# A hybrid state-space and attention layer on one core: three queues put into the written order

## The chip, the cores and the metric

The kernel runs on one core of one Trainium2 chip. A core has five instruction queues that run beside each other: TensorE (PE, matrix multiplications, with its weight loads listed as PEld), VectorE (DVE), ScalarE (ACT), GpSimd (POOL) and SyncE (SP). SP does no arithmetic here: it issues nearly all transfers (DMA) between the memory of the chip and the core's own buffers. An instruction that has to wait for another engine or for a transfer holds up everything behind it in its queue. The metric is the device time of one execution in microseconds (us).

## The reference

One layer of a streaming encoder, sequence length 2048, width 1024, all float32:

```python
h = rmsnorm(x, norm_mix_g)
proj = h @ w_in 
y_ssm = s5_mixer(u_ssm, ...)
y_att = chunked_attention(q, k, v, attn_rel_bias)
mixed = concat([rmsnorm(y_ssm, g1), rmsnorm(y_att, g2)])
x = x + mixed @ w_out
h2 = rmsnorm(x, norm_ffn_g)
x = x + (silu(h2 @ w_gate) * (h2 @ w_up)) @ w_down
return rmsnorm(x, norm_final_g)
```

The state-space mixer has 32 groups of 16 channels with 64 complex states each, scanned in time, followed by GELU and a gate. The attention has 8 heads of 64 dimensions; a frame sees its own chunk of 64 frames and the 8 chunks before it, with a learned bias by distance.

## The kernel before

Products of float32 are made from three products of a rounded high part and a low remainder (hi times hi, hi times lo, lo times hi). So every operand is split: ACT casts the high part, DVE or POOL subtracts it to get the low part (the function `split`).

The program has these phases: a prologue that projects u and prepares the state-space tables; the attention stage (`att_phase`), which is what the change touches; the mixing phase with w_out; gate and up projections; the down projection.

The attention stage is written as 128 steps: four quarters of the sequence (`sb`, 512 frames each), four pairs of heads (`pr`), two heads (`hh`), four blocks of queries (`qp`). `ORDER = "sptf"` says what a step writes: the scores of this step with the row minimum and the exponential ("s"; scores carry a minus sign, so the minimum is the maximum of softmax); at the end of a head its product with the values ("p"); the transposition of the probabilities of two steps earlier, and their split into `pth` (ACT copy) and `ptl` (DVE subtraction) ("t"); and last pieces of filler work ("f"). Filler work comes from generators, each wrapped in a `Unit` with the steps between which its pieces are spread; a unit is started `pre` (2 or 3) steps ahead so that its first piece, its loads, is written early:

- `hT_unit` loads tiles of x, transposed (`xt`, two buffers in quarters 1 to 3), scales them on DVE, casts `hi` on ACT and subtracts `lo` on DVE. The first three k-tiles have a second set of buffers (`hi0x` to `lo2x`), and are prepared by a unit of their own, earlier.
- `qk_unit` makes q and k of one pair of heads: first q (eight k-tiles), then k. The results are copied into `q2h`, `q2l` and `k2`; half of q2h and q2l goes to the other partitions by a transfer, k is stored in `ks`, and the k of the quarter before is loaded from there.
- `v_unit` makes the values of four heads from two weight tiles; k-tiles 4 to 7 use the second.
- `ssm_unit` (eight of them, 15 steps each) does one block of state-space groups: it loads `U`, `Bst`, `Tm` and `Vm`, multiplies, scans on POOL, multiplies again and stores `y` with eight transfers.

The weights of these units come in `load_w`: in quarter 0 as `raw` (two buffers) followed by a split and a store of the split pair to `wss` (`keep_w`); in quarters 1 to 3 as the split pair from `wss` (1 MB per tile, three buffers `w`). `load_nb` loads the bias tile `nb` of a head. `pv_scale` scales the result of a pair of heads and stores it in `ya_s`.

The order on the engines: TensorE's instructions keep the order in which they are written (`k.ta`). An instruction written through `k.V`, `k.A` or `k.Q` (DVE, ACT, SP) keeps its order among those written in the same way. All others are placed by the compiler's scheduler, which may issue them long before the place where they are written, if buffers are free. In the attention stage before, only a few are pinned: those of quarter 0's input tiles, and the first pair of weights.

Of the kernel before, what the change touches and what calls it, by code (L numbers as in the profile page):

```python
# [16 lines left out]
P = 128  # L17
# [62 lines left out]
class Pinned:  # L80


    def __init__(self, tc, eng):
        self.tc, self.eng = tc, eng

    def __getattr__(self, name):
        f = getattr(self.eng, name)
        return lambda *a, **b: self.tc.keep_in_program_order(f(*a, **b))


class K:
    def __init__(self, tc, io):
        self.tc, self.nc, self.io = tc, tc.nc, io
        self.n = 0
        self.te = Ordered(tc)
        self.ta = self.te if PINA else tc.nc.tensor
        self.V, self.A, self.Q = (Pinned(tc, e) for e in (tc.nc.vector, tc.nc.scalar, tc.nc.sync))
# [9 lines left out]
def f32(ap):  # L107
    return ap.bitcast(F32)
# [451 lines left out]
def ssm_unit(k, p, psum, S, b, eng):  # L560
# [5 lines left out]
    def load(out, in_):  # L566
        ins = nc.sync.dma_start(out, in_)
        if b == 0:
            k.tc.keep_in_program_order(ins)

# [72 lines left out]
    for q in range(GP):  # L643
        ps = k.t(psum, "pj", [P, 2, NC], bufs=2)
        for g2 in range(2):
            g = 2 * q + g2
            k.ta.matmul(ps[:, g2, :], tm[:, g, :], U[:, g, :], start=True, stop=False)
            k.ta.matmul(ps[:, g2, :], vm[:, g, :], XG[:, g, :], start=False, stop=True)
        nc.scalar.copy(Y[:, 2 * q : 2 * q + 2, :], ps[:])
        if q == GP - 1:  # L650
            for j in range(L):
                nc.sync.dma_start(S["y"][b * F : (b + 1) * F, j, :].rearrange("(g c) t -> c g t", c=CH), Y[j * CH : (j + 1) * CH])
        yield
# [27 lines left out]
def att_phase(k, ident, S):  # L681
    tc, nc, io = k.tc, k.nc, k.io
    with ExitStack() as cx:
# [3 lines left out]
        def load_w(sb, n):  # L687

            w = k.t(aw, "w", [P, 2, 1024], F32R, bufs=WB)
            if sb == 0:  # L690
                raw = k.t(aw, "raw", [P, 1024], bufs=2)
                pin = n in (0, 4)
                (k.Q if pin else nc.sync).dma_start(raw[:], io["w_qk"][n] if n < 8 else io["w_v"][n - 8])
                split(k, w[:, 0], w[:, 1], raw[:], k.V if pin else k.wlo_eng, k.A if pin else None)
                keep[n] = w
            else:
                nc.sync.dma_start(f32(w[:]), S["ws"][n])
            return w[:, 0], w[:, 1]

        def keep_w(n):  # L700
            if n in keep:
                (k.Q if n in (0, 4) else nc.sync).dma_start(S["ws"][n], f32(keep.pop(n)[:]))

        def hT_unit(sb, q0=0, q1=KT):
            hi, lo = hT.setdefault(sb, ([], []))
            ts = slice(sb * SB, (sb + 1) * SB)
            xts = {}
            V, A, Q = (k.V, k.A, k.Q) if sb == 0 else (nc.vector, nc.scalar, nc.sync)

            def load(q):  # L710
                if q < q1:
                    x = RING[q] if sb == 0 and q < 2 * DB else None
                    xts[q] = k.t(aw, x, [P, SB]) if x else k.t(aw, "xt", [P, SB], bufs=XB)
                    Q.dma_start(xts[q][:], io["xt"][q * P : (q + 1) * P, ts])

            ahead = 2 if sb else KT
            for q in range(q0, q0 + ahead):
                load(q)
            def low(q):
                V.tensor_tensor(lo[q][:], xts[q][:], f32(hi[q][:]), op=ALU.subtract)  # L720

            for q in range(q0, q1):
                yield
                load(q + ahead)
                xt = xts[q]
                for v, n in zip(hT[sb], ("hi", "lo")):
                    v.append(k.t(aw, f"{n}{q}x" if q < DB and sb % 2 else f"{n}{q}", [P, SB], F32R))
                V.scalar_tensor_tensor(xt[:], xt[:], k.gm[:, q : q + 1], S["rsn"][:, ts], op0=ALU.mult, op1=ALU.mult)
                A.copy(hi[q][:], xt[:])  # L729
                if sb == 0 and q:  # L730
                    low(q - 1)
                if sb or q == KT - 1:
                    low(q)
            yield

        def qk_unit(sb, pr):
# [7 lines left out]
            qk[sb, pr] = ts  # L744
            if sb > 0:
                for hh in range(2):
                    nc.sync.dma_start(f32(ts[hh][2][:, :SB]), S["k"][(sb - 1) % 2, 2 * pr + hh])
            both = (sb, pr) == (0, 0)
            pss = []
            for c in range(2):  # L750
# [13 lines left out]
                for hh in range(2):  # L764
# [3 lines left out]
                    if c == 0:  # L768
                        nc.scalar.activation(q2h[a, :], ps[a, :], AF.Copy, scale=-0.125)
                        nc.vector.scalar_tensor_tensor(q2l[a, :], ps[a, :], -0.125, f32(q2h[a, :]), op0=ALU.mult, op1=ALU.subtract)  # L770
                        nc.sync.dma_start(f32(q2h[o, :]), f32(q2h[a, :]))
                        nc.sync.dma_start(f32(q2l[o, :]), f32(q2l[a, :]))
                    else:
                        nc.scalar.copy(k2[a, -SB:], ps[a, :])
                        nc.vector.tensor_tensor(k2[o, -SB:], ps[a, :], f32(k2[a, -SB:]), op=ALU.subtract)
                        if sb < NSB - 1:
                            nc.sync.dma_start(S["k"][sb % 2, 2 * pr + hh], f32(k2[:, -SB:]))
                yield
# [36 lines left out]
        def load_nb(h):  # L815
            nb = k.t(aa, "nb", [P, 640], bufs=2)
            nc.sync.dma_start(nb[:], S["nbm"][h])
            return nb

        def scores(st):  # L820
# [23 lines left out]
            if (hh, qp) == (0, 0):  # L844
# [46 lines left out]
        def pv_scale(st):  # L891
# [6 lines left out]
            nc.vector.tensor_tensor(ya[:], ya[:], pb[:], op=ALU.mult)  # L898
            nc.sync.dma_start(S["ya"][sb, pr * P : (pr + 1) * P, :], ya[:])

# [30 lines left out]
        psum2 = cx.enter_context(tc.tile_pool(name="aps2", bufs=1, space=bass.MemoryType.PSUM, reuse_waits="tile"))  # L931
        units = []
        for sb in range(NSB):
# [13 lines left out]
        for s in range(N + LAG + 2):  # L947
            if s == OPEN:
                aw.release()
                mix = mix_phase(k, S, lambda: k.t(pfs, "pf", [P, 512]))  # L950
# [3 lines left out]
            for o in ORDER:  # L954
                if o == "s" and s < N:
                    scores(steps[s])
                elif o == "t" and LAG <= s < N + LAG:
# [747 lines left out]
```

## Time and profile before

| | |
|---|---|
| median of 3 runs | 2314.3 us (2306.25 to 2315.94) |
| the profiled execution | 2304.9 us, its span 2303.1 us, mean granted clock of TensorE 0.975 |
| TensorE busy | 2183.8 us, 95% of the span |
| DVE, ACT, POOL busy | 1487.8, 1001.3 and 1061.0 us |
| DMA | 437 MB, 190 GB/s on average |
| attention stage | steps from about 143 us to about 745 us |

How to read the rows. A row of the waits says which instruction of TensorE waited (tile, line), for what (engine or DMA, tile, line), and then: microseconds in total, how often, the longest. A row of the timeline has the start, the duration, the engine, the line, the operation, out<-in and the count, and in brackets the idle time before it with what ended it. A row of the windows has the stretch, its length, and then the busy time (and instructions) of PE, PEld, DVE, ACT and POOL, the granted TensorE clock (1 is full speed), the busy share of the DMA engines and GB/s. A row of the DMA issues has out<-in, the queue, the count, the size and the median time from issue to landing. A row of a group has the shape, the count, the busy time, the mean in ns, and the idle time before with its cause. Names are those of the program; SPq is SP's queue.

### The profile page before, as it was taken

How to read it: one execution, taken by the hardware profiler on the slowest of the kernel's cores; microseconds unless marked ns; L12 is line 12 of the kernel's file. 1: busy time of each engine (PE TensorE's matmuls, PEld its weight loads, DVE VectorE, ACT ScalarE, POOL GpSimd, SP SyncE). 2: the span in 40 equal slices, each digit the busy share in tenths (PEclk: the TensorE clock that was granted, in tenths of full speed). 3: DMA queues.
4: the chain of work that ended last, by engine and by line, in shares of the span. 5: the costliest groups of instructions: out<-in, count | busy, mean ns of one | idle time of the engine just before them, and what ended most of it. 6: DMA issues, size and time to landing. Idle time of an engine off the chain costs nothing.

```text
span 2303.1 us, 30454 instructions
## 1 busy us (share of the span) xinstructions
PE 2183.8 (95%) x10568; PEld 1834.1 (80%) x10568; DVE 1487.8 (65%) x2286; ACT 1001.3 (43%) x1675; POOL 1061.0 (46%) x1245
## 2 busy tenths in 40 slices
PE   8978799999997899989999999999999999999997
PEld 6667688898986788778888887888888878888886
DVE  7845555656555756676775669766645376578676
ACT  6335555555557542343333335333333343344332
POOL 3416655455660433265555554555555314445442
PEclk9989999999998999999999999999999999999998
DMA  8788766766653534754554556555433287465552
GB/s 295 260 286 265 235 210 204 207 190 193 192 137 114 178 118 163 249 165 143 167 193 157 205 190 254 195 193 167 158 96 110 76 326 265 165 228 183 201 182 74
DMA packets 216370, 437.00 MB, mean 190 GB/s; under 512 B 27352, under 2 KB 58120, under 8 KB 209112
## 3 DMA queue, kind: packets, MB, share of 16 engines
q1 hardware_dynamic: 211352, 420.89, 55.0%
q0 software_dynamic: 4864, 14.17, 1.9%
q8 instruction: 83, 1.36, 0.2%
q14 instruction: 71, 0.58, 0.1%
HBM read 294.98 MB, written 132.15 MB: 185 GB/s over the span
## 4 chain that ended last, share of the span: by engine, by line
PE 59%; DVE 3%; DMA 1%; ACT 1%; issue 1%; POOL 1%; SPq 0%; DVEq 0%; ACTq 0%; POOLq 0%
PE X L74 20%; PE ps L74 18%; PE Y L74 10%; PE big L74 6%; PE W L74 5%; DVE acc L1575 1%; DMA lo<-hc 0%; DMA x<-xt 0%; DVE xt L1117 0%; DVE lo L166 0%; DVE hd L166 0%; POOL c L166 0%; ACT hi L165 0%; POOL sa L1125 0%; DMA gl<-x 0%
## 5 line engine op out<-in xcount | busy, mean ns | idle before, releaser
L74 PE MATMUL X<-hi,c 128*128 128x512 f32 x1408 | 452.2, 392 | 7.6 <-ACT u L1391 3.5
L74 PE MATMUL ps<-hd,hd 128*128 128x512 f32 (+1 forms) x1968 | 431.7, 381 | 3.9 <-DVE hd L166 3.7
L74 PEld LDWEIGHTS ps<-hd,hd 128*128 128x128 f32 x1968 | 358.8, 190 | 75.5 <-DVE hd L166 5.1
L166 POOL TENSOR_TENSOR c<-S,c 128x512 fp32r<-128x512 f32 x176 | 253.1, 1440 | 260.7 <-ACT c L165 258.8
L74 PEld LDWEIGHTS X<-hi,c 128*128 128x128 f32 x1408 | 265.8, 189 | 65.2 <-ACT u L1391 5.1
L74 PE MATMUL X<-lo,c 128*128 128x512 f32 x704 | 275.3, 391 | 0.0
L166 POOL TENSOR_TENSOR hd<-hd 128x1536 fp32r<-128x1536 f32 (+1 forms) x46 | 159.1, 3463 | 232.0 <-ACT hd L165 218.8
L166 POOL TENSOR_TENSOR c<-raw,c 128x512 fp32r<-128x512 f32 x132 | 189.0, 1432 | 137.5 <-ACT c L165 109.1
L165 ACT CAST hd<-hd 128x1536 fp32r<-128x1536 f32 (+1 forms) x106 | 147.4, 1393 | 219.4 <-DMA hd<-hq 134.5
L74 PE MATMUL Y<-hi,c 128*128 128x512 f32 x704 | 225.5, 391 | 4.8 <-DVE u L1395 4.8
L1521 DVE TENSOR_TENSOR acc<-acc,ps 128x512 f32<-128x512 f32 x196 | 129.2, 681 | 79.5 <-PE ps L74 79.1
L74 PE MATMUL big<-m,woh 128*128 128x512 f32 x512 | 165.4, 404 | 0.6 <-DVE m L166 0.4
L165 ACT CAST c<-S 128x512 fp32r<-128x512 f32 x176 | 109.5, 622 | 116.5 <-PE Y L74 59.1
L74 PE MATMUL pf<-hi,w 128*128 128x512 f32 x416 | 150.9, 415 | 9.4 <-ACT hi L729 5.8
L74 PEld LDWEIGHTS Y<-hi,c 128*128 128x128 f32 x704 | 132.6, 188 | 33.9 <-DVE u L1395 6.3
L74 PEld LDWEIGHTS X<-lo,c 128*128 128x128 f32 x704 | 133.0, 189 | 27.7
L1391 ACT COPY u<-X 128x512 f32<-128x512 f32 x132 | 77.1, 585 | 177.5 <-PE X L74 177.5
L846 DVE CUSTOM_DVE_ANT_0 s<-sc,nb 128x640 f32<-128x640 f32 (+4 forms) x128 | 94.4, 737 | 89.4 <-PE sc L74 85.9
L605 POOL TENSOR_TENSOR st<-X,a 128x128 f32<-128x128 f32 (+2 forms) x136 | 47.4, 349 | 220.0 <-ACT X L591 157.4
L165 ACT CAST c<-raw 128x512 fp32r<-128x512 f32 x132 | 82.1, 622 | 143.1 <-PE Y L74 80.3
L166 DVE TENSOR_TENSOR hd<-hd 128x1536 fp32r<-128x1536 f32 (+1 forms) x60 | 119.3, 1990 | 31.2 <-ACT hd L165 30.5
L74 PE MATMUL Y<-lo,c 128*128 128x512 f32 x352 | 137.2, 390 | 0.0
(462 smaller groups left out, 4644.2 us busy)
## 6 DMA issues: line engine op xcount, KB each, us to landing
w<-wss SPq DMA_DIRECT2D x36, 1024.0 KB, 5.5
hq<-g SPq DMA_DIRECT2D x140, 256.0 KB, 2.1
hd<-hq SPq DMA_DIRECT2D x42, 768.0 KB, 4.5
hd<-wc SPq DMA_DIRECT2D x42, 768.0 KB, 6.0
raw<-in_w_gate SPq DMA_DIRECT2D x44, 512.0 KB, 3.7
raw<-in_w_up SPq DMA_DIRECT2D x44, 512.0 KB, 4.1
wc<-px SPq DMA_DIRECT2D x66, 256.0 KB, 3.2
wss<-w SPq DMA_DIRECT2D x12, 1024.0 KB, 5.6
```

The costliest lines, as they stand in the source:

```text
L74: return self.tc.keep_in_program_order(self.tc.nc.tensor.matmul(*a, **b))
L165: (hi_eng or nc.scalar).copy(hi, raw)
L166: (lo_eng or nc.gpsimd).tensor_tensor(lo, raw, f32(hi), op=ALU.subtract)
L605: eng.tensor_tensor(t[:, :, :, :n], src, ar, op=ALU.mult)
L846: nc.vector.tensor_tensor_reduce(s[:, :nk].rearrange("p (a b) -> p a b", a=nch), ps[:, :nch, :half], hd.nb[:, nk - 1 :: -1].rearrange("p ( ...
L1391: nc.scalar.copy(u[:], ps[:])
L1521: V.tensor_tensor(a, a, ps[:], op=ALU.add)
L1575: nc.vector.scalar_tensor_tensor(v, v, k.go[:, i : i + 1], self.rs[:, : self.n], op0=ALU.mult, op1=ALU.mult)
```

## The change

In the attention stage every transfer issued by SP, the weight splits, the input tiles of all quarters and ACT's copies of the state-space blocks are written through `k.Q`, `k.V` and `k.A`, so that they keep the written order among themselves. Three things are written at another place: the loads of input tiles in quarters 1 to 3 come behind the subtraction that frees the buffer; the load of the old k comes behind the q2h and q2l copies of its head; and the exponential of a step is issued in the step's filler part, behind the copy and subtraction of the probabilities transposed in that step. The exponentials, the transposition's copies, the scores' DVE instruction and the q/k/v evacuations are still placed by the scheduler. From step 119 on (`OPEN`) the class flag `free` turns the pinning off. Later phases pin only four copies of w_down tiles to `wt`; they are not pinned any more.

```diff
 class Pinned:
+    free = False
     def __getattr__(self, name):
         f = getattr(self.eng, name)
-        return lambda *a, **b: self.tc.keep_in_program_order(f(*a, **b))
+        return f if self.free else lambda *a, **b: self.tc.keep_in_program_order(f(*a, **b))
...
     def load(out, in_):
-        ins = nc.sync.dma_start(out, in_)
-        if b == 0:
-            k.tc.keep_in_program_order(ins)
+        k.Q.dma_start(out, in_)
...
-                nc.scalar.copy(X[g2 * NS : (g2 + 1) * NS, c, q, :], ps[c * NS : (c + 1) * NS, g2, :])
+                k.A.copy(X[g2 * NS : (g2 + 1) * NS, c, q, :], ps[c * NS : (c + 1) * NS, g2, :])
...
             if sb == 0:
-                pin = n in (0, 4)
-                (k.Q if pin else nc.sync).dma_start(raw[:], io["w_qk"][n] if n < 8 else io["w_v"][n - 8])
-                split(k, w[:, 0], w[:, 1], raw[:], k.V if pin else k.wlo_eng, k.A if pin else None)
+                k.Q.dma_start(raw[:], io["w_qk"][n] if n < 8 else io["w_v"][n - 8])
+                split(k, w[:, 0], w[:, 1], raw[:], k.V, k.A)
             else:
-                nc.sync.dma_start(f32(w[:]), S["ws"][n])
+                k.Q.dma_start(f32(w[:]), S["ws"][n])
...
-            V, A, Q = (k.V, k.A, k.Q) if sb == 0 else (nc.vector, nc.scalar, nc.sync)
+            V, A, Q = (k.V, k.A, k.Q)
...
-                load(q + ahead)
+                if sb == 0:
+                    load(q + ahead)
...
+                if sb:
+                    load(q + ahead)
...
-            if sb > 0:
-                for hh in range(2):
-                    nc.sync.dma_start(f32(ts[hh][2][:, :SB]), S["k"][(sb - 1) % 2, 2 * pr + hh])
...
+                        k.Q.dma_start(f32(q2h[o, :]), f32(q2h[a, :]))
+                        k.Q.dma_start(f32(q2l[o, :]), f32(q2l[a, :]))
+                        if sb > 0:
+                            k.Q.dma_start(f32(k2[:, :SB]), S["k"][(sb - 1) % 2, 2 * pr + hh])
...
-            nc.scalar.activation(s[:, :nk], s[:, :nk], AF.Exp, bias=mn[:], scale=-1.0, accum_out=sums[sb, pr][:, hh, qp : qp + 1])
+            acc = sums[sb, pr][:, hh, qp : qp + 1]
+            return lambda: nc.scalar.activation(s[:, :nk], s[:, :nk], AF.Exp, bias=mn[:], scale=-1.0, accum_out=acc)
...
             if s == OPEN:
+                Pinned.free = True
...
                 elif o == "f":
+                    if exps:
+                        exps.pop()()
                     for u in units:
                         u.advance(s)
```

The loads and stores of `raw`, `wss`, `nb`, `ya_s`, `ks` and `y` change in the same way from `nc.sync` to `k.Q`.

On TensorE and POOL the two programs have the same instructions in the same order. On SP, DVE and ACT they differ within the attention stage; SP differs beside that by the four `wt` copies, which now stand among the first loads of the program. Three places on SP follow. The first is the end of quarter 0, from the last V weights to the second state-space block. Before:

```order
L693 DMA raw_2321<-in_w_v 128x1024
L771 DMA q2h_2110<-q2h_2110 64x512
L772 DMA q2l_2111<-q2l_2111 64x512
L693 DMA raw_2326<-in_w_v 128x1024
L567 DMA Bst_2623<-bsts_71 128x512
...
L899 DMA ya_s_66<-ya_2047 128x512
...
L693 DMA raw_2605<-in_w_qk 128x1024
L693 DMA raw_2610<-in_w_qk 128x1024
...
L652 DMA y_65<-X_2546 16x4x256 x8
L567 DMA U_2614<-u_64 16x4x256 x7
```

and now:

```order
L89 DMA ya_s_66<-ya_2046 128x512
L89 DMA raw_2321<-in_w_v 128x1024
L89 DMA raw_2326<-in_w_v 128x1024
...
L89 DMA y_65<-X_2546 16x4x256 x8
L89 DMA raw_2605<-in_w_qk 128x1024
L89 DMA raw_2610<-in_w_qk 128x1024
L89 DMA U_2614<-u_64 16x4x256 x8
L89 DMA Bst_2623<-bsts_71 128x512
L89 DMA Tm_2625<-kts_80 16x4x128 x8
```

The V weights (raw_2321, raw_2326) moved behind the store of ya, the last q/k weights of the quarter (raw_2605, raw_2610) behind the eight stores of y, and Bst from far ahead to behind its block's U loads.

The second place is the weight pair of the first V unit of quarter 1 (w_3211, w_3213). Before:

```order
L697 DMA w_3211<-wss_75 128x2048
L714 DMA xt_2987<-in_xt 128x512
L567 DMA Bst_3422<-bsts_71 128x512
L714 DMA xt_4382<-in_xt 128x512
L714 DMA xt_4384<-in_xt 128x512
L697 DMA w_3213<-wss_75 128x2048
L747 DMA k_773_2999<-ks_68 128x512
L771 DMA q2h_2994<-q2h_2994 64x512
L772 DMA q2l_2995<-q2l_2995 64x512
L771 DMA q2h_2997<-q2h_2997 64x512
```

and now:

```order
L89 DMA q2h_2994<-q2h_2994 64x512
L89 DMA q2l_2995<-q2l_2995 64x512
L89 DMA k_770_2996<-ks_68 128x512
L89 DMA q2h_2997<-q2h_2997 64x512
L89 DMA q2l_2998<-q2l_2998 64x512
L89 DMA k_773_2999<-ks_68 128x512
L89 DMA ya_s_66<-ya_2858 128x512
L89 DMA w_3211<-wss_75 128x2048
L89 DMA w_3213<-wss_75 128x2048
```

The pair moved behind the copies, the loads of the old k and a store of ya; the input tiles of quarter 2 (xt_4382, xt_4384) and the Bst of a later block no longer stand there. The third place is the last q/k unit of quarter 1 and the input tiles of quarter 2. Before:

```order
L697 DMA w_4559<-wss_75 128x2048
L771 DMA q2h_4422<-q2h_4422 64x512
L772 DMA q2l_4423<-q2l_4423 64x512
L771 DMA q2h_4425<-q2h_4425 64x512
L772 DMA q2l_4426<-q2l_4426 64x512
L747 DMA k_1156_4737<-ks_68 128x512
L714 DMA xt_4714<-in_xt 128x512
L714 DMA xt_4721<-in_xt 128x512
```

and now:

```order
L89 DMA q2h_4425<-q2h_4425 64x512
L89 DMA q2l_4426<-q2l_4426 64x512
L89 DMA k_1076_4427<-ks_68 128x512
L89 DMA w_4557<-wss_75 128x2048
L89 DMA w_4559<-wss_75 128x2048
L89 DMA nb_4579<-nbms_69 128x640
L89 DMA xt_4630<-in_xt 128x512
L89 DMA xt_4632<-in_xt 128x512
L89 DMA ks_68<-k_1073_4424 128x512
L89 DMA ks_68<-k_1076_4427 128x512
L89 DMA xt_4719<-in_xt 128x512
```

xt_4630 and xt_4632, which stood some 45 rows earlier, are now behind the weight pair of quarter 2, and the next input tile behind both stores of k.

More of the change, by code (lines that the diff above doesn't have):

```diff
@@ L94, in __init__ @@
         self.n = 0
+        Pinned.free = False
         self.te = Ordered(tc)
@@ L648, in ssm_unit @@
             k.ta.matmul(ps[:, g2, :], vm[:, g, :], XG[:, g, :], start=False, stop=True)
-        nc.scalar.copy(Y[:, 2 * q : 2 * q + 2, :], ps[:])
+        k.A.copy(Y[:, 2 * q : 2 * q + 2, :], ps[:])
         if q == GP - 1:
             for j in range(L):
-                nc.sync.dma_start(S["y"][b * F : (b + 1) * F, j, :].rearrange("(g c) t -> c g t", c=CH), Y[j * CH : (j + 1) * CH])
+                k.Q.dma_start(S["y"][b * F : (b + 1) * F, j, :].rearrange("(g c) t -> c g t", c=CH), Y[j * CH : (j + 1) * CH])
         yield
@@ L701, in keep_w @@
             if n in keep:
-                (k.Q if n in (0, 4) else nc.sync).dma_start(S["ws"][n], f32(keep.pop(n)[:]))
+                k.Q.dma_start(S["ws"][n], f32(keep.pop(n)[:]))
         def hT_unit(sb, q0=0, q1=KT):
@@ L770, in qk_unit @@
                         nc.vector.scalar_tensor_tensor(q2l[a, :], ps[a, :], -0.125, f32(q2h[a, :]), op0=ALU.mult, op1=ALU.subtract)
-                        nc.sync.dma_start(f32(q2h[o, :]), f32(q2h[a, :]))
-                        nc.sync.dma_start(f32(q2l[o, :]), f32(q2l[a, :]))
+                        k.Q.dma_start(f32(q2h[o, :]), f32(q2h[a, :]))
+                        k.Q.dma_start(f32(q2l[o, :]), f32(q2l[a, :]))
+                        if sb > 0:
+                            k.Q.dma_start(f32(k2[:, :SB]), S["k"][(sb - 1) % 2, 2 * pr + hh])
                     else:
@@ L776, in qk_unit @@
                         if sb < NSB - 1:
-                            nc.sync.dma_start(S["k"][sb % 2, 2 * pr + hh], f32(k2[:, -SB:]))
+                            k.Q.dma_start(S["k"][sb % 2, 2 * pr + hh], f32(k2[:, -SB:]))
                 yield
@@ L816, in load_nb @@
             nb = k.t(aa, "nb", [P, 640], bufs=2)
-            nc.sync.dma_start(nb[:], S["nbm"][h])
+            k.Q.dma_start(nb[:], S["nbm"][h])
             return nb
@@ L931, in att_phase @@
         psum2 = cx.enter_context(tc.tile_pool(name="aps2", bufs=1, space=bass.MemoryType.PSUM, reuse_waits="tile"))
-        units = []
+        units, exps = [], []
         for sb in range(NSB):
@@ L955, in att_phase @@
                 if o == "s" and s < N:
-                    scores(steps[s])
+                    exps.append(scores(steps[s]))
                 elif o == "t" and LAG <= s < N + LAG:
```

2 lines of the change are left out of this document (1 added, 1 removed).

## The prediction

> **What bounds the kernel now.** I read the page first (busy time, then the chain that ended last), then the stretch that the change touches, by windows, then who kept TensorE waiting there.
>
> ```profile
> PE 2183.8 (95%) x10568; PEld 1834.1 (80%) x10568; DVE 1487.8 (65%) x2286; ACT 1001.3 (43%) x1675; POOL 1061.0 (46%) x1245
> 150.00:330.00 180.00, 154.57 (x876) 133.09 (x877) 98.23 (x223) 94.57 (x233) 94.88 (x217) 0.95 0.75 235
> ```
>
> TensorE is busy 95% of the span, and it sets the end. The attention stage lies roughly between 143 and 745 us, and its first 180 us after the start are loose: 154.57 of them busy, while the DMA engines are busy 0.75 of the time. TensorE's instruction order is the same in both kernels, so the only question is how much later or earlier each operand arrives. These are its waits between 150 and 790 us:
>
> ```profile
> PE pt L77 <- DVE ptl L865: 13.5, 10, 2.6
> PE sc L74 <- DVE k L775: 6.8, 3, 2.9
> PE pf L74 <- ACT hi L729: 5.8, 2, 3.5
> PE sc L74 <- DVE mn L846: 5.6, 4, 3.3
> PE pj L74 <- DMA U<-u: 4.3, 2, 2.7
> PE pf L74 <- ACT w L165: 3.6, 1, 3.6
> PE pj L74 <- DMA Tm<-kts: 1.8, 2, 1.1
> ```
>
> No row here says that a projection waited for a weight pair of quarters 1 to 3, and the state-space blocks waited 6.1 us in all. Transfers are hidden, because SP issued them far ahead. The written order takes that lead away at the places below.
>
> **The change part by part.** The sum is made against the profiled run, 2304.9 us. That is 9.4 us under the median of the runs shown (2314.3), so I add what the sum gives to the median.
>
> *Term 1, the raw weights of quarter 0.* SP's rows around 200 us, and the landing times of the transfers:
>
> ```profile
> 187.98 0.98 SPq L693 DMA_DIRECT2D raw<-in_w_v  x1
> 202.31 0.32 SPq L899 DMA_DIRECT2D ya_s<-ya  x1
> 210.64 1.87 SPq L693 DMA_DIRECT2D raw<-in_w_qk  x2
> 225.15 3.61 SPq L652 DMA_DIRECT2D y<-X  x8
> raw<-in_w_qk SPq DMA_DIRECT2D x8, 512.0 KB, 7.7
> raw<-in_w_v SPq DMA_DIRECT2D x4, 512.0 KB, 9.3
> xt<-in_xt SPq DMA_DIRECT2D x26, 256.0 KB, 4.1
> w<-wss SPq DMA_DIRECT2D x36, 1024.0 KB, 5.5
> U<-u SPq DMA_DIRECT2D x64, 64.0 KB, 2.5
> Bst<-bsts SPq DMA_DIRECT2D x8, 256.0 KB, 4.2
> L165 ACT CAST w<-raw x4: 1044/1050/1053, 197.9 to 227.4; 128x1024 fp32r<-128x1024 f32 x4
> 207.78 0.48 PE L74 MATMUL pf<-w,hi 128*128 128x256 f32 x2
> 231.35 0.48 PE L74 MATMUL pf<-hi,w 128*128 128x512 f32 x1
> ```
>
> Site A: the V weights now stand behind the store of ya, which cannot issue before 202.31, because it waits for the scaled rows. They issue at about 202.7; a transfer of this size takes between the 4.1 of a small xt tile and its own 9.3, and the cast 1.05. So the weight is ready between 207.8 and 213.0, against its first use at 207.78: a stall of 0 to 5.3. Site B: the last raw pair of quarter 0 stood at 210.64 and now stands behind eight y stores, which end at 228.8. With 4.1 to 7.7 for landing and 1.05 for the cast it is ready at 233.9 to 237.6, against 231.35: 2.5 to 6.2. I take 8 for both together (bounds 2.5 and 11.5); the queue is full there (0.75), so neither lands at its fastest.
>
> *Term 2, Bst behind U.* Bst was issued long before its block. Now it follows the eight U loads, and then Tm: it lands 0.4 + 4.2 - 2.5 = 2.1 later than the last U, which was the last to arrive. Of the seven later blocks four already wait for U or Tm (two and two in the rows above), so each of those pays the 2.1 in full: 8.4, and I take 9. Bounds: 0 (if the blocks begin later anyway) and 7 x 2.1 = 15.
>
> *Term 3, the normed input at the start of quarters 1, 2 and 3.* There are two xt buffers, so the written chain is a round of load, DVE scaling, ACT cast, DVE subtraction. Quarter 1 already ran like that:
>
> ```profile
> 261.95 0.79 PE L74 MATMUL pf<-hi,w 128*128 128x512 f32 x1 [3.45 <-ACT hi L729]
> 269.24 0.50 PE L74 MATMUL pf<-hi,w 128*128 128x512 f32 x1 [2.30 <-ACT hi L729]
> L728 DVE SCALAR_TENSOR_TENSOR xt<-xt,g_mix,rsn 128x512 f32<-128x512 f32 x24 | 20.1, 840 | 11.0 <-DMA xt<-in_xt 10.8
> L720 DVE TENSOR_TENSOR lo<-xt,hi 128x512 fp32r<-128x512 f32 x18 | 17.4, 974 | 2.6 <-ACT hi L729 2.5
> L729 ACT CAST hi<-xt 128x512 fp32r<-128x512 f32 x18 | 11.2, 619 | 15.6 <-DVE xt L728 13.4 <-PE pf L74 1.9
> ```
>
> These two stalls, 5.75 together, are the whole of the row "ACT hi L729: 5.8, 2", so quarters 2 and 3 paid nothing. In the written order their loads stand behind the weight pair and the q2h, q2l and k2 transfers, as in quarter 1. One round is 4.1 + 0.84 + 0.62 + 0.97 = 6.5 us. I give quarters 2 and 3 what quarter 1 paid, 2 x 5.75 = 11.5, and quarter 1 itself 4.5 more, since its loads now also follow the weight pair of 2 MB (2.1 MB at the 235 GB/s of the first window is 8.9 us of transfer, about half of it past the lead): 16. Bounds 0 and 3 x 6.5 = 19.5.
>
> *Term 4, the weight pairs of quarters 1 to 3.* These now follow the copies of the unit before. The gates and the first uses, in the kernel before:
>
> ```profile
> 275.32 0.58 SPq L899 DMA_DIRECT2D ya_s<-ya  x1
> 281.41 0.48 PE L74 MATMUL pf<-w,hi0x 128*128 128x256 f32 x2
> 564.89 4.82 SPq L652 DMA_DIRECT2D y<-X  x8
> 573.36 0.48 PE L74 MATMUL pf<-w,hi0x 128*128 128x256 f32 x2
> 637.35 0.37 SPq L899 DMA_DIRECT2D ya_s<-ya  x1
> 637.76 0.48 PE L74 MATMUL pf<-w,hi0x 128*128 128x256 f32 x2
> ```
>
> First V unit of quarter 1: ya ends at 275.9, the two k2 loads now ahead of it add 0.8, the first weight lands 0.4 + 5.5 later, at 282.6 against 281.41 (1.2). A second megabyte behind it needs about 4.5 more at 235 GB/s and its first use is only 1.5 us after the unit's start, so about 4 in all. First V unit of quarter 3: y ends at 569.7, the weight lands at 575.6 against 573.36 (2.2, and with the second about 5). Last V unit of quarter 3: ya at 637.7, so 643.6 against 637.76, 5.9, plus the second's share, 7.5. Last V unit of quarter 1 stands like the first: 4. The q/k pairs need their second weight only half a unit later and mostly fit. The list gives 20; the units themselves begin later behind other stalls, which delays uses and gates alike, so I take 15. Bounds 0 and 20.
>
> *What is gained.* The first bias tile of the stage now issues ahead of two 1 MB weight stores, so this stall goes, 3.3:
>
> ```profile
> 152.59 0.55 PE L74 MATMUL sc<-hi2x,hi0x 128*128 128x256 f32 x1 [3.34 <-DVE mn L846]
> 204.00 0.87 PE L77 MATMUL pt<-ident,s 128*128 128x128 f32 x3 [1.81 <-DVE ptl L865]
> 200.00:210.00 10.00, 7.87 (x42) 6.66 (x41) 6.58 (x17) 5.63 (x14) 8.90 (x26) 0.83 0.86 313
> 235.47 1.96 PE L74 MATMUL pj<-U,Bst 128*128 128x256 f32 x8 [1.14 <-DMA Tm<-kts]
> 230.00:240.00 10.00, 8.86 (x48) 7.36 (x47) 3.12 (x10) 4.99 (x15) 0.29 (x1) 1.00 0.55 137
> ```
>
> Far-ahead casts and scalings no longer run in front of a step's copies on DVE and ACT: of the 13.5 (ptl), 6.8 (k) and remaining 2.3 (mn) I take 5 back; bounds 0 and 20. The exponential behind the split of step s-2 lets ptl start earlier and costs nothing while its own result is used two steps later (steps are (745 - 143) / 128 = 4.7 us long); if that cover went, it would cost about one exponential per step. The k2 loads behind q2h/q2l are used half a unit later, also 0. The copies of four W_down tiles that drop into the prologue are priced among the rivals.
>
> *The clock.* A stall of 1.81 us at 204.00 is followed by a granted clock of 0.83 over 10 us, which is 3.4 us at half speed, so 1.7 us of work lost; the stall of 1.14 at 235.47 left it at 1.00. The terms above add some ten stalls of about 2 us or more and take one away; several fall in one slow stretch, so I take 6 x 1.7 = 10. Bounds 0 and 17.
>
> The Trainium skill ("TensorE: Matmul & The Clock Gate", section "HAM oscillation — how this bites in real kernels") states the rule that gaps above about 3.4 us drop the clock. By it only the new stalls that may pass 3.4 us (site A, site B and the last V unit) would pay, 3 x 1.7 = 5, and the sum would be 45 and not 50. The trace disagrees at 204.00, where 1.81 us was enough, and the sum goes by the trace.
>
> **Sum:** 8 + 9 + 16 + 15 - 3.3 - 5 + 10 = 50. The profiled execution would be at about 2355, the median at 2314 + 50 = 2364.
>
> **The rivals.** *The order frees DVE and ACT, and the loads stay hidden* (faster). Each unit starts its loads two or three steps ahead, 9.4 to 14 us; an ordinary landing plus cast is 5.5 + 1.05. If the lead covers it everywhere, what remains is the removal of jams: the rows ptl, k, hi, w and mn are 35.3 us, of which two thirds, about 25, could go: 2290. It decides from the point where no written gate (ya, y, q2h) holds SP for longer than 3 us past the lead. For it: these waits are the largest. Against it: sites A and B, where the gate is known to the microsecond. *No net change:* landings shorten, because fewer transfers are in flight, and terms 1 to 4 come to the 8 gained: 2314. For it: one loaded queue (0.75) now carries no far-ahead tiles; against it: the gates are waits for compute, not for bandwidth. *All upper bounds:* 11.5 + 15 + 19.5 + 20 - 3.3 + 17 = 80, so 2394 and a little more if they feed each other. *The W_down copies hurt the prologue:*
>
> ```profile
> 70.00:80.00 10.00, 10.00 (x45) 8.11 (x44) 6.46 (x10) 7.19 (x13) 6.13 (x11) 0.97 0.95 359
> 80.00:90.00 10.00, 9.76 (x44) 7.44 (x43) 9.18 (x37) 6.47 (x10) 2.40 (x4) 1.00 0.40 117
> ```
>
> 2 MB more are read and written there, 4 MB at 359 GB/s, some 12 us of a share that is 0.95 in one window and 0.40 in the next; I price it at 0, since the slack behind 80 us takes it, with 7 above. By itself that would be 2321.
>
> **How the numbers follow.** About 0.5% (11.6 us) is what a measurement of this kernel can tell from no change. My forecast, slower by 25 to 80, has a chance of 0.68, with its own range 2338 to 2394. Worse than that: 0.08. Near no change, the prologue's case among it: 0.13 (0.10 within the bound, 0.03 above it). Faster: 0.11. So slower 0.79, same 0.10, faster 0.11. The range reaches from 2312, which leaves out the faster case and some of the middle one, to 2395, which leaves out most of the worst one.
>
> **What would show it.** In the profile after: a wait of TensorE for the cast of w near 208 and near 231 (term 1), waits for DMA Bst (term 2), waits for hi and lo at three quarters and not one (term 3), waits for DMA w<-wss, in the V units above all (term 4), no 3.34 at the stage's start, and lower clocks behind each. TensorE's busy time would grow by the clock's part alone. I am wrong if the rows for DMA w and Bst stay near nothing, or if the ptl and k rows shrink by more than 20.

## The result

The changed kernel takes 2372.06 us (median of 4 runs, 2365.26 to 2374.86), the kernel before 2310.28 us in the same comparison. The ratio is 1.0262, with a 95% interval of 1.0231 to 1.0293: it is slower by 2.6%, or 62 us. The forecast was 2364 with a range of 2312 to 2395, a growth of 50 us counted from a median of 2314. The profiled execution took 2373.1 us, with a span of 2371.0 us and a mean granted clock of 0.965 (2304.9, 2303.1 and 0.975 before).

TensorE's instructions are the same in both programs and in the same order, so the two traces can be laid on each other. This is how much later the same TensorE instruction starts in the changed kernel, for the first one at or after the time given in the kernel before:

| start before (us) | 140 | 200 | 250 | 300 | 350 | 400 | 500 | 600 | 650 | 700 | 750 | 1000 | 2290 |
|---|---|---|---|---|---|---|---|---|---|---|---|---|---|
| later by (us) | 0.0 | -4.4 | 6.9 | 15.9 | 31.5 | 34.1 | 42.0 | 54.5 | 64.7 | 64.5 | 64.0 | 64.6 | 67.9 |

The whole loss arises between 200 and 650 us, in the attention stage, in steps. The prologue, which now also copies four W_down tiles, is unchanged (0.0 at 140 us). Of the last 4 us 3.5 come between 900 and 1200 us. The two runs below that edit the kernel before, with those copies at their old place, fall behind it by 3.0 and 2.3 us in the same stretch, so this is no sign of a cost of the copies.

### The profile after

The busy line of the page, and the waits of TensorE between 150 and 860 us, the stretch that answers to 150 to 790 before:

```profile
PE 2202.9 (93%) x10568; PEld 1844.4 (78%) x10568; DVE 1488.6 (63%) x2286; ACT 1003.4 (42%) x1675; POOL 1064.0 (45%) x1245
PE pf L74 <- DMA w<-wss: 20.9, 8, 5.8
PE sc L74 <- DVE mn L847: 16.3, 11, 2.4
PE pj L74 <- DMA Tm<-kts: 12.3, 4, 5.8
PE pf L74 <- ACT w L89: 11.8, 3, 4.7
PE pf L74 <- ACT hi L89: 10.8, 7, 3.6
PE pt L77 <- DVE ptl L867: 5.8, 6, 2.3
PE sc L74 <- DVE k L776: 4.3, 3, 1.7
PE pf L74 <- DVE lo L89: 3.1, 7, 1.2
PE pf L74 <- DVE w L89: 2.3, 4, 0.9
```

Operands that come by SP's queue have replaced those of the engines at the head of the list. Weight pairs, which nobody waited for, now cost 20.9 us. The rows for ptl and k are smaller, as was hoped for by the faster rival. All rows of this stretch together, the smaller ones left out above included, are 104.5 us, against 59.6 before: 44.9 more. Beside that TensorE's busy time grew by 19.1, from 2183.8 to 2202.9, for the same instructions: a slower clock.

The windows of the stage, before and after, say the same. Before:

```profile
150.00:745.00 595.00, 542.44 (x3241) 482.43 (x3242) 341.49 (x657) 333.80 (x683) 294.08 (x706) 0.96 0.65 196
```

After, up to the point that answers to it (five instructions more), and one window around a stall:

```profile
150.00:810.00 660.00, 562.44 (x3246) 492.49 (x3247) 343.43 (x655) 335.88 (x684) 297.95 (x706) 0.93 0.57 178
204.00:214.00 10.00, 7.12 (x33) 6.69 (x34) 3.98 (x4) 3.17 (x5) 8.35 (x10) 0.57 0.99 357
```

The lowest clock that a short window shows is 0.50 (205 to 210 us), so a slow stretch runs at half speed. A mean clock of 0.96 over 595 us is about 48 us of that, and 0.93 over 660 us about 92: 44 us more at half speed, which loses 22 us of work. The growth of the busy time here, 20.0 us, fits. The 0.57 in the window that begins in the stall of site A is 8.6 us at half speed, not 3.4.

Where TensorE stood, site by site (the timeline; in brackets the idle time ahead):

```profile
205.99 0.58 PE L74 MATMUL pf<-w,hi 128*128 128x256 f32 x1 [4.65 <-ACT w L89]
235.20 0.50 PE L74 MATMUL pf<-hi,w 128*128 128x512 f32 x1 [3.43 <-ACT w L89]
268.98 0.79 PE L74 MATMUL pf<-hi,w 128*128 128x512 f32 x1 [3.65 <-ACT hi L89]
297.69 0.65 PE L74 MATMUL pf<-w,hi0x 128*128 128x256 f32 x2 [4.95 <-DMA w<-wss]
327.35 3.75 PE L74 MATMUL pj<-U,Bst 128*128 128x256 f32 x8 [5.82 <-DMA Tm<-kts]
375.23 0.79 PE L74 MATMUL pf<-w,hi0x 128*128 128x256 f32 x2 [2.46 <-DMA w<-wss]
380.13 0.80 PE L74 MATMUL pf<-w,hi 128*128 128x256 f32 x2 [1.97 <-DMA w<-wss]
403.11 3.18 PE L74 MATMUL pj<-U,Bst 128*128 128x256 f32 x8 [2.23 <-DMA Tm<-kts]
700.03 0.79 PE L74 MATMUL pf<-w,hi0x 128*128 128x256 f32 x2 [5.84 <-DMA w<-wss]
```

And SP's queue ahead of the stall at 327.35:

```profile
310.01 3.61 SPq L89 DMA_DIRECT2D y<-X  x8
313.71 2.26 SPq L89 DMA_DIRECT2D w<-wss  x2
316.03 8.25 SPq L89 DMA_DIRECT2D U<-u  x8
324.38 0.37 SPq L89 DMA_DIRECT2D Bst<-bsts  x1
324.79 3.90 SPq L89 DMA_DIRECT2D Tm<-kts  x8
```

Bst is issued at 324.38. Wherever the trace has the landing of a Bst, it is 2.8 to 3.4 us after the issue, so this one is there at 327.2 to 327.8: TensorE resumes at 327.35. The row names Tm, which is another transfer that had just landed; by the times it is Bst that was awaited. There is a second thing to see: the eight U loads took 8.25 us to issue, where the eight y stores ahead took 3.61 and the U loads of the next block 3.65. They stand behind two weight tiles of 1 MB each. The trace shows what they waited for. Among SP's transfers, none starts before the one eight places ahead of it has landed: this holds for all 935 in each of the 14 traces of this case for which that landing is recorded, and the closest starts 0.016 us behind it. The last U load is such a case:

```profile
323.97 0.30 SPq L89 DMA_DIRECT2D U<-u  x1
```

The second weight tile, eight places ahead and issued at 315.64, landed at 323.96. So one slow transfer on SP holds back the issue of what stands eight places behind it.

### The profile page after: what moved, and what is told of

It reads as the page before. It is cut to its first block, busy times and chain, and to the rows that moved or that the text cites. A ratio compares the mean times of both kernels' runs of the same rounds, so it can differ in the third digit from the quotient of the medians.

```text
span 2371.0 us, 30406 instructions
## 1 busy us (share of the span) xinstructions
PE 2202.9 (93%) x10568; PEld 1844.4 (78%) x10568; DVE 1488.6 (63%) x2286; ACT 1003.4 (42%) x1675; POOL 1064.0 (45%) x1245
## 4 chain that ended last, share of the span: by engine, by line
PE 56%; DVE 4%; DMA 2%; POOL 1%; issue 1%; ACT 1%; SPq 0%; DVEq 0%; ACTq 0%; POOLq 0%
PE X L74 19%; PE ps L74 17%; PE Y L74 10%; PE big L74 5%; PE W L74 5%; DMA lo<-hc 1%; DVE lo L168 1%; DVE acc L1580 1%; DMA x<-xt 0%; DVE xt L1122 0%; DMA hc<-gh 0%; POOL c L168 0%; DMA yr<-y 0%; DVE hd L168 0%; POOL sa L1130 0%
## 5 line engine op out<-in xcount | busy, mean ns | idle before, releaser
L74 PE MATMUL pf<-hi,w 128*128 128x512 f32 x416 | 154.0, 421 | 19.6 <-ACT hi L89 10.8
```

The lines of the kernel that those rows point to most:

```text
L74: return self.tc.keep_in_program_order(self.tc.nc.tensor.matmul(*a, **b))
```

## The experiments

My theory was that SP's written order makes loads late, at the four places of the prediction. The rivals were that DVE's and ACT's order or the later exponential costs the time, and, from the first results on, that the waits only move when one load is mended. All ratios are against the kernel before on the same chip.

### SP's order taken back

```diff
-        k.Q.dma_start(out, in_)
+        (k.Q if b == 0 else nc.sync).dma_start(out, in_)
```

Every `k.Q` that the change brought goes back to `nc.sync`, or to the few pinned ones of before. The later places of the input tiles' loads and of the load of the old k stay, here and in the next run.

> The changed kernel, but SP's transfers of the attention stage are placed by the scheduler again, as before; DVE and ACT keep the written order, and the exponential stays behind the split. Theory (SP's written order makes the loads late, and that is nearly the whole loss): 2300 to 2318 us, the waits for DMA w and Tm fall from 20.9 and 12.3 us to under 2 and under 8. Rival (the order on DVE and ACT costs it): above 2345.

2327.44 us, ratio 1.0063 (1.0046 to 1.008). The wait for DMA w is gone and the one named after Tm fell to 7.0. So 45 of 62 us came back, but not all: 16 us stay. The two waits fell as expected, while the time lies between the theory's 2300 to 2318 and the rival's 2345. The waits of TensorE say where:

```profile
PE pf L74 <- ACT hi L89: 15.0, 9, 3.8
PE sc L74 <- DVE mn L847: 7.8, 5, 4.3
PE pj L74 <- DMA Tm<-kts: 7.0, 4, 3.4
```

The delay against the kernel before, in the profiled executions 23 us at the end, grows from 1.4 to 10.8 us between 240 and 270, from 11.2 to 14.2 between 400 and 420, and from 15.1 to 20.2 between 540 and 560: there the input tiles of the three later quarters are first used.

### SP's order alone

```diff
-                split(k, w[:, 0], w[:, 1], raw[:], k.V, k.A)
+                split(k, w[:, 0], w[:, 1], raw[:], k.V if n in (0, 4) else k.wlo_eng, k.A if n in (0, 4) else None)
...
-            return lambda: nc.scalar.activation(...AF.Exp...)
+            nc.scalar.activation(...AF.Exp...)
```

The state-space copies and the input tiles of later quarters go back to `nc.scalar` and `nc.vector` in the same way; SP stays in the written order.

> The changed kernel, but DVE's and ACT's instructions are placed by the scheduler as before and the exponential is written at its old place: of the change only SP's written order is left. Theory (SP's order): 2355 to 2375 us, waits for DMA w near 21. Rival (order on DVE and ACT): under 2325.

2373.48 us, ratio 1.0265 (1.025 to 1.028), as in the changed kernel. SP's order alone makes the whole loss, as the theory had it. Together with the first run this also shows that the parts don't add: SP alone costs 62 us, the rest alone 16, and both together 62. I take it that the late input tiles are paid once, whichever of the queues makes them late; the row for hi is 10.8 us in the changed kernel, 10.5 here and 15.0 in the first run.

```profile
PE pf L74 <- DMA w<-wss: 19.3, 8, 7.5
PE sc L74 <- DVE mn L847: 18.2, 11, 3.2
PE pf L74 <- ACT w L167: 13.0, 3, 5.0
```

### The exponential back at its place

The lambda is called in `scores`, as above; the rest is the changed kernel.

> The changed kernel with the exponential back at its old place, in the scores. Theory (the exponential's place is hidden): 2364 to 2380 us, the wait for mn near 16. Rival (the later exponential holds the scores' buffers and makes the new waits for mn): 2355 to 2362, the mn row under 6.

2372.98 us, ratio 1.0267 (1.0243 to 1.029), with 15.3 us of waits for mn. The later exponential costs nothing and brings nothing, and it doesn't make the waits for mn.

### Bias tiles sooner

```diff
-            if qp == 2 and (sb, h) < (NSB - 1, H - 1):
+            if qp == 0 and (sb, h) < (NSB - 1, H - 1):
                 nbs[(h + 1) % H] = load_nb((h + 1) % H)
```

In the changed kernel DVE's scores instruction stood idle for the bias tile eight times (a row of that line's waits):

```profile
  DMA nb<-nbms: 7.2, 8
```

> The changed kernel, but the bias tile of the next head is loaded at the first step of a head and not at its third. Theory (the mn waits, 16.3 us, come from bias tiles that now stand behind weight pairs): the mn row falls under 6 and the time to 2355 to 2364 us. Rival (the mn waits come from the order on DVE): mn stays near 16, time 2367 to 2376.

2369.53 us, ratio 1.0251 (1.0236 to 1.0266). The cause of the wait is shown: the mn row fell from 16.3 to 3.1, where the rival expected 16. But the gain that I expected from it, 8 to 17 us, did not come; the time is 2.5 us lower, less than the runs scatter. All rows of the list together fell by 7.3 us, from 104.5 to 97.2, but TensorE's busy time in the profiled execution rose from 2202.9 to 2212.2, at a slower clock. The rest of the 13 us appears again in other rows, in these above all:

```profile
PE pf L74 <- DMA w<-wss: 24.0, 10, 6.7
PE pf L74 <- ACT hi L89: 13.7, 8, 5.9
PE pf L74 <- ACT w L89: 13.3, 4, 4.9
PE sc L74 <- DVE mn L847: 3.1, 3, 1.2
```

### Input tiles as before

```diff
-            V, A, Q = (k.V, k.A, k.Q)
+            V, A, Q = (k.V, k.A, k.Q) if sb == 0 else (nc.vector, nc.scalar, nc.sync)
...
-                if sb == 0:
-                    load(q + ahead)
+                load(q + ahead)
...
-                if sb:
-                    load(q + ahead)
```

> The changed kernel, but the input tiles of quarters 1 to 3 are as before (loads, scaling, cast and subtraction placed by the scheduler, the next load ahead of the subtraction). Theory (term 3): the waits for hi and lo fall from 13.9 us to about 6, and with their slow clock the time to 2356 to 2364 us. Rival (the wait only moves to the next late operand, as it did when the bias tiles were advanced): 2367 or more, although hi and lo fall.

2359.26 us, ratio 1.0211 (1.0191 to 1.0231): some 12 us less than the changed kernel, as expected. hi and lo fell from 13.9 to 9.7 us, not to the 6 of the expectation; the wait for weights fell too:

```profile
PE pf L74 <- DMA w<-wss: 16.8, 10, 5.0
PE pf L74 <- ACT hi L728: 6.9, 4, 3.6
PE pf L74 <- DVE lo L719: 2.8, 3, 1.8
```

### SP's order and the input tiles taken back

Two edits together, that of the first experiment and that of the one above.

> The kernel with SP's transfers placed by the scheduler (2327 us), and beside that the input tiles of quarters 1 to 3 as before on DVE and ACT. What is left of the change is the order of the weight splits and state-space copies, and the later exponential. Theory (the 16 us left there are the input tiles' order, which the waits for hi, 15.0 us against 5.8, and the steps at the quarters' starts suggest): 2306 to 2316 us. Rival (they are the weight splits or the later exponential): 2322 to 2330.

2314.14 us, ratio 1.0017 (1.0004 to 1.0031). Of the 16 us that were left without SP's order, 12 are the input tiles' order on DVE and ACT with the later place of their loads, and the row for hi is back near the 5.8 of before:

```profile
PE pf L74 <- ACT hi L728: 6.2, 2, 3.8
```

What remains of the change then, the order of the splits and of the state-space copies and the later exponential, costs some 4 us (1 to 7 by the interval).

### Weights sooner, in the written order

```diff
+        for (s0, _, _), (_, sb, a) in zip(order, order[1:]):
+            early[s0 + (1 if sb else 0)] = [(sb, n) for n in (a[:1] if sb else a)]
...
                 elif o == "f":
+                    for a in early.get(s, ()):
+                        early_w(*a)
```

`order` lists the units in turn with their first step, their quarter and their weight tiles. About one unit ahead, `early_w` issues through `k.Q` both raw tiles in quarter 0 and the first tile of the pair later; the splits and the second tiles stay where they were.

> The changed kernel, still in the written order, but the loads of weights are written earlier: in quarter 0 both raw tiles, in quarters 1 to 3 the first tile of each pair, about one unit ahead. Theory (terms 1 and 4: what counts is the place on SP): the waits for DMA w fall from 20.9 to under 10 and those for the cast of w from 11.8 to about 4, the time to 2345 to 2358 us. Rival (waits only move): 2366 or more.

2354.76 us, ratio 1.0199 (1.0175 to 1.0222): 17 us less than the changed kernel. Nothing but the place of loads on SP was altered, and with it the time at which they take their buffers. The wait for the cast of w is gone from the list, that for DMA w was halved (10.6, just above the 10 expected), while the state-space blocks wait longer:

```profile
PE pj L74 <- DMA Tm<-kts: 17.2, 6, 6.3
PE pf L74 <- DMA w<-wss: 10.6, 3, 5.6
```

### Bst ahead of U

```diff
+    load(bst[:].rearrange("p g m -> p (g m)"), S["bst"][...])
     for j in range(L):
         load(U[j * CH : (j + 1) * CH], ...)
-    load(bst[:].rearrange("p g m -> p (g m)"), S["bst"][...])
```

> The changed kernel, but each state-space block loads Bst ahead of its eight U tiles instead of behind them. Theory (term 2: TensorE resumes about 3 us after the issue of Bst, whatever transfer the wait is put down to): the 12.3 us of waits named after Tm fall to 5 or less, the time to 2360 to 2367 us. Rival (the last U tiles, held by the eight transfers in flight, bind as late): the row stays above 9, time 2368 or more.

2367.12 us, ratio 1.0245 (1.023 to 1.026): 5 us less, between the two expected times and within the scatter of the changed kernel's runs. The row fell from 12.3 to 9.2 only, as the rival had it:

```profile
PE pj L74 <- DMA Tm<-kts: 9.2, 4, 3.9
```

In the changed kernel the last U had landed 1.0 to 1.3 us before TensorE resumed, in the three of these four blocks where its landing is recorded, and Bst came last; here it landed 0.2 and 0.5 us before, in the two where it is recorded. So Bst behind U is a part of that wait, about a quarter; the U tiles themselves, which stand behind weights and y stores, are the larger part.

### Four places mended

The last edits together: weights sooner, Bst ahead of U, bias tiles sooner, input tiles as before.

> The changed kernel with four places mended: first weights of a pair one unit earlier, input tiles of quarters 1 to 3 as before, bias tiles two steps earlier, Bst ahead of U. SP otherwise keeps the written order. Theory (the parts add: 17 from weights, 13 from input tiles, 7 from Bst, 3 from bias tiles): 2328 to 2340 us. Rival (mended loads push others back on the one queue): 2345 or more.

2342.57 us, ratio 1.0127 (1.0104 to 1.0149). Singly the four brought 17, 5, 3 and 12 us, 37 together; jointly 29. By the ratios it is 33 and 31, and each interval reaches 3 to 7 us to either side, so this run does not settle whether the four add. The time lies between the two expected ranges, 2 to 3 us from each. The list of waits is headed by the state-space loads and by second weight tiles:

```profile
PE pj L74 <- DMA Tm<-kts: 17.7, 7, 6.1
PE pf L74 <- DMA w<-wss: 14.6, 4, 7.3
```

### And the state-space loads freed

```diff
-        k.Q.dma_start(out, in_)
+        (k.Q if b == 0 else nc.sync).dma_start(out, in_)
```

> The mended kernel (2343 us) with, beside that, the loads of the state-space blocks after the first one (U, Bst, Tm, Vm) placed by the scheduler as before. Theory (what is left there are mostly these loads, 17.7 us of waits named after Tm against 1.8 plus 4.3 for U in the kernel before, and some slow clock): that row at 8 or less, 2322 to 2332 us. Rival (the waits move to the weight pairs, 14.6 us there, and the rest is spread over the queue): the row falls, but the time stays at 2337 or more.

2332.65 us, ratio 1.0089 (1.0064 to 1.0114): 10 us less. The row named after Tm fell to 9.6, not to 8, and the time lies at the upper edge of the expectation:

```profile
PE pf L74 <- DMA w<-wss: 14.3, 4, 6.9
PE pj L74 <- DMA Tm<-kts: 9.6, 3, 6.2
```

So the freed loads were about a third of what was left, and weight pairs (14.3) are the largest row of the rest. The 6.2 us in the other row are the first block, whose loads are still in the written order here; it waits as long in the run before (6.1 us), where its U loads stand behind a raw weight that was moved ahead and are issued from 171.46 on, not from 157.59 as in the changed kernel. There the rival was right: one load mended, another pushed back. What the last 21 us consist of beyond these rows was not taken apart.

### Two attempts on the kernel before

One writes the first bias tile of the stage in order, ahead of two weight stores:

```diff
-            nc.sync.dma_start(nb[:], S["nbm"][h])
+            (k.Q if not st_head else nc.sync).dma_start(nb[:], S["nbm"][h])
...
-                (k.Q if n in (0, 4) else nc.sync).dma_start(S["ws"][n], f32(keep.pop(n)[:]))
+                (k.Q if n in (0, 4, 8, 10) else nc.sync).dma_start(S["ws"][n], f32(keep.pop(n)[:]))
```

> The kernel before, with only the first bias tile of the attention stage written in order ahead of the two weight stores of the first V unit (the stores are pinned for it). Theory (the 3.3 us stall of the stage's start is that load, and 1.7 us of slow clock hang on it): 3 to 5 us faster than before, 2305 to 2308 us. Rival (the load is not what the scores wait for, or the gain is lost later): within 2 us of before.

2311.55 us, ratio 1.0011 (1.0 to 1.0021): no gain. The tile was issued at 144.11, ahead of both stores, and the stall was there all the same:

```profile
144.11 0.44 SPq L817 DMA_DIRECT2D nb<-nbms  x1
144.60 1.65 SPq L88 DMA_DIRECT2D wss<-w  x2
151.95 0.55 PE L74 MATMUL sc<-hi2x,hi0x 128*128 128x256 f32 x1 [3.95 <-DVE mn L846]
```

So the place ahead of the stores is not what cures it. The tile was hardly sooner, since the kernel before issued it at 144.45, and it landed at 151.36, some 7 us later. In the changed kernel it was issued at 142.46 and landed 3.5 us later, and the stall shrank from 3.34 to 1.22; there the raw tile and the input tile that precede the bias tile here (at 142.88 and 143.26) stand elsewhere as well. Which of them holds the bias tile up was not tried.

The other begins the later input tiles one step sooner, `HTS = -9, -7` in place of `-8, -6`.

> The kernel before, with the later input tiles of quarters 1 to 3 begun one step sooner. It tests whether the largest remaining load wait of the kernel before (hi at the start of quarter 1, 5.8 us and 1.7 us of slow clock) can be had by an earlier place. Theory (the place is what counts): hi under 2, 2303 to 2307 us. Rival (the two xt buffers and the full queue set it): within 2 us of before or slower.

2313.48 us, ratio 1.0012 (1.0002 to 1.0022). The wait for hi went from 5.8 to 5.0 us only, and that for lo from 0.2 to 1.8. An earlier place does not help; that the two buffers and the queue set the pace is likely, but not shown. No version that I ran beats the kernel before.

## Why the prediction was right

Its direction and mechanism held: the loss is SP's written order (the second experiment alone reproduces it), at the sites that the rows of before named. The time, 2372, is 8 above the forecast; as a growth it is 62 us where 50 was forecast, since the kernel before was at 2310 here and not at 2314. By terms:

| step of the prediction | forecast (us) | measured (us) |
|---|---|---|
| 1, raw weights of quarter 0 | 8 | 8.1 at the two sites (4.65 and 3.43); their row 3.6 to 11.8; beside it DVE w 0 to 2.3 |
| 2, Bst behind U | 9 | waits for U and Tm 6.1 to 12.3, +6.2; undoing it alone: 5, within the scatter |
| 3, input tiles | 16 | waits for hi and lo 6.0 to 13.9, +7.9; undoing it: 12 |
| 4, weight pairs | 15 | 0 to 20.9; weights sooner (with term 1): 17 |
| first bias tile, and jams on DVE | -8.3 | ptl and k 21.1 to 12.0, -9.1; mn 5.6 to 16.3, +10.7 |
| slow clock | 10 | busy time in the stage +20.0 |
| sum | 50 | 62 (median), 68 (the profiled execution) |

That the sum comes so near is in part luck. By these rows terms 2 and 3 were some 11 us too high together; term 4, the bias tiles and the clock were some 26 too low.

**Terms 1 and 4** came out nearly site by site. Site A was given 0 to 5.3 and took 4.65; site B 2.5 to 6.2 and took 3.43. The V units were priced at about 4, 4, 5 and 7.5; the first of quarter 1 took 4.95, the last of quarter 1 2.46 + 1.97, the first of quarter 3 2.83 and the last 5.84 + 1.07. One wait, 1.78 us at 540.32 in quarter 2, was not on the list. All eight waits for weights fall in V units, none in the q/k units, as was argued from the second weight's early use. What held is the gate: in all four units the pair is issued right behind the ya or y store that the prediction named. The landings held less well: the first tile of these pairs took 4.8 to 9.3 us, not 5.5 each time. In the first V unit of quarter 1 the first tile alone, with its 9.3, made the whole stall, where the prediction had 1.2 for it and the rest for the second. That the price of this unit comes out is luck.

**Term 3** was right in kind, though by the first experiment the order on DVE and ACT makes these tiles late even without SP's. The waits themselves are smaller than I gave (many of about 1 us instead of two long ones), and their undoing is worth more than these rows show: the wait for weights fell with them, and a slow clock may hang on them.

**Term 2** is partly right. I priced only Bst's own delay. The larger part is that U stands behind weights and y stores: eight U loads took 8.25 us to issue where 3.65 is seen too, since the last of them could not start before the second weight tile had landed.

**The step that failed** is the bias tile. I took the first one's stall as a gain of 3.3 us and did not ask where the other 31 would stand. In the written order many of them stand behind weight pairs and block loads, DVE waited for eight of them (7.2 us), and the row for mn trebled. As a cost it is smaller than the row says: with these waits gone the time fell by 2.5 us only, because other operands were waited for instead and the clock was slower.

The other half of this term, the jams on DVE and ACT, shrank for another reason than the one given. The prediction put it down to casts and scalings that no longer run in front. But with SP's order alone, where DVE and ACT are placed by the scheduler, the rows for ptl and k come to 13.0 us, nearly the 12.0 of the changed kernel, against 21.1 before. So the order on SP is enough for it; by what way was not tried.

**The clock** was mis-sized by half. I took six slow stretches of 3.4 us, 20 in all; the windows show 44 us more at half speed. Some of the stretches were longer: 0.57 from 204 to 214 us, around the stall of 4.65, and 0.55 from 702 to 712, behind the one of 5.84. The stall of 4.95 left 0.83 (296 to 306), about 3.4 us at half speed. The Trainium skill ("TensorE: Matmul & The Clock Gate", section "HAM oscillation — how this bites in real kernels") gives gaps above some 3.4 us as the condition. By it the surcharge would have been 5 with the stalls that were forecast, and an estimated 8.5 with those of the trace (eight above 3.4 in the two windows of the stage shown above against three before, 1.7 for each of the five more). The trace disagrees here as it did before: in the window behind the stall of 2.23 us at 403.11 the granted clock was 0.83. In that behind the one of 1.78 us at 540.32 it was 1.00, but so it was behind 2.35 us at 630.73, so the length of one stall alone does not decide it here.

```profile
402.00:412.00 10.00, 8.89 (x48) 8.16 (x49) 2.32 (x4) 5.30 (x13) 3.85 (x8) 0.83 0.81 289
539.00:549.00 10.00, 8.69 (x66) 8.51 (x67) 3.50 (x7) 3.25 (x7) 0.00 (x0) 1.00 0.62 179
628.00:638.00 10.00, 7.65 (x57) 7.25 (x56) 2.66 (x7) 5.84 (x15) 2.87 (x6) 1.00 0.74 212
```

**The rivals.** The faster one had its facts right: the rows for ptl and k did shrink, by 9.1 us. It fails on its condition, that no written gate holds the loads past their lead. No change by shorter landings is refuted: the DMA share fell from 0.65 to 0.57, over a longer stage, and the raw tiles between 150 and 260 us still took 6.2 to 6.8 us to land where it is recorded (3.9 to 7.8 before). The W_down copies cost the prologue nothing that the alignment shows.

## What to carry to other kernels

A queue in program order turns the wait of one instruction into a delay of all that are written behind it: SP's order alone cost 62 us here. Before pinning a queue, list for each load the instruction written ahead of it, the time at which the trace shows that instruction could issue, and the load's first use; look also at what stands eight places ahead, if the trace shows such a limit. The jams that went away with the far-ahead issue (9 us here) are much less than what that issue hides. The waits are not a sum of independent prices: SP's order costs 62 us and the rest of the change 16, but both together 62, and without the late bias tiles 13 us of one row went away and only 2.5 of the time. So sizes must be measured by undoing parts together as well as singly.

## What was not expected of the hardware

The granted clock costs about a third of the loss (20 of 62 to 68 us), from many stalls of 1 to 6 us, and around some of them it stayed low for most of 10 us. In no trace here did SP start a transfer before the one eight places ahead had landed, so transfers behind two of 1 MB take longer to issue, not only to land: eight loads of 64 KB took 8.25 us, 7.00 ahead of the stall at 630.73 and 10.04 ahead of that at 707.59. The wait's name can mislead: the four waits named after Tm ended 3.0 to 3.6 us after the issue of Bst, which takes 2.8 to 3.4 to land. That U was hardly earlier is what the run with Bst ahead of U showed.

```profile
694.26 10.04 SPq L89 DMA_DIRECT2D U<-u  x8
704.34 0.42 SPq L89 DMA_DIRECT2D Bst<-bsts  x1
707.59 3.60 PE L74 MATMUL pj<-U,Bst 128*128 128x256 f32 x8 [1.92 <-DMA Tm<-kts]
```
